# Runs of eight equal products in the half blocks, evenly issued background steps, and decay operands moved to ScalarE, in a two-layer hybrid trunk

## The chip, the cores and the metric

The kernel runs on one core of a Trainium2 chip, as one launch. The figure of merit is the device time of one execution in microseconds (us). The profile names the engines of a core: PE is TensorE (matrix products; its weight loads are listed apart as PEld), DVE is VectorE, ACT is ScalarE, POOL is GpSimd, and SP issues most of the DMA transfers. Each engine works through its own queue of instructions in order; where it needs a result of another engine, it waits on a semaphore, and everything behind the waiting instruction in its queue waits as well. PSUM is the memory into which PE accumulates.

## The reference, cut to what matters

The input is 256 tokens of 2048 features. Layer A is a gated delta-rule layer, layer B is chunked attention over the token's own chunk and the chunks before it. Both have 16 heads of 128 features, and both are wrapped the same way:

```python
# layer A (chunks of 64 tokens)
proj = h @ w_in                                   # 2048 x 8224: q, k, v, z, a, b
qkv  = silu(causal_depthwise_conv(proj[..., :6144], conv_w))
q, k = l2_norm(q) * 128 ** -0.5, l2_norm(k)
g    = -exp(a_log) * softplus(a + dt_bias);  gc = cumsum(g)      # within a chunk
decay = exp(where(tril, gc_i - gc_j, -inf))
lower = where(strict tril, (k * beta) @ k.T * decay, 0)
sol   = solve_triangular(eye + lower, [v * beta, k * beta * exp(gc)])
# a scan over the 4 chunks with a 128 x 128 state per head gives o
out   = h + (rms_norm(o) * silu(z)) @ w_out
# layer B
proj = h @ w_in                                   # 2048 x 8192: q, k, v, z
out  = h + (softmax(q @ k.T * scale + bias) @ v * silu(z)) @ w_out
```

Everything is single precision. The four weight matrices make nearly all of the arithmetic and of the traffic.

## The kernel before, in words

**Products.** PE multiplies numbers of a shorter type, fp32r. A weight `w` is therefore split into `hi = cast(w)` and `lo = w - hi`, the activations likewise into `xh` and `xl`, and a product of the reference is three on PE: hi·xh, hi·xl and lo·xh. The weights stream through the core in chunks of 512 KB, in the order of a list, `plan`. `fetch()` (L171 to L206) prepares a chunk: SP starts the transfer into `wt` (L198, four buffers), ACT casts it to `whi` (L199, three buffers), DVE subtracts to get `wlo` (L200, three buffers). A chunk is fetched three chunks ahead of its use, but a `whi` buffer can be written only when PE has done the last product that reads the chunk three before it.

**Kinds of block.** A "half" block makes 256 features for all 256 tokens from four chunks. Each chunk holds four slices (`j`) of the contraction and two sets of 128 features (`s`). For each pair (s, j) there are two products: a long one of 512 columns, hi·[xh|xl] (L247), and a short one of 256 columns, lo·xh (L250), which adds to the first half of the same accumulator. `features2` writes them in groups of two slices, four long and then four short ones. "tokens" blocks (L256 to L258) make 512 features of 256 tokens in products of 512 columns, "features" blocks (L237 to L240) in products of 256 columns. Blocks accumulate in PSUM tiles named `psp`, of which there are two buffers. When a half block is done, `joined` (L299 to L306) queues a copy of one half of it on ACT (L303) and the addition of the other half on DVE (L304); the addition frees the `psp` buffer for the block after the next.

**Order of the work.** What stands between the blocks (normalisation, convolutions, decays, the inversion of the triangular matrices, the scan, attention) is written as generators, in two lists `bgq` and `bg2`. After every slice or group the chunk loop calls `step(rate)`, which resumes one of them up to its next `yield`. A scheduler then fixes the order of each engine's queue when the kernel is built; the orders shown below are those that it fixed.

**Decays** (L392 to L494). For each of four groups of heads, `rhs` (L457 to L464) multiplies a triangular matrix by the high and the low parts of `g`: the high parts on DVE, the low parts on POOL, each one instruction of 128x512 per half. Products (L475) sum them; `tail` (L479) and three exponentials (L480, L481, L483) follow on DVE and ACT, and L490 multiplies.

**Convolution** (L494 to L505): `raw` is `ev` times a norm (L319), ACT multiplies by the first tap (L501), DVE adds the other taps (L503). **Inversion** (L596 to L697): eight copies on ACT (L610), transposes of 32x32 pieces on DVE (L620), then runs of small products on PE (L650, L670, L672). L560 are the products of keys with keys ahead of it, L706 writes a piece of the value path.

Of the kernel before, what the change touches and what calls it, by code (L numbers as in the profile page):

```python
# [23 lines left out]
NWARM = 12  # L24
TIE0 = 4
TIE = 2
GROUP = 2


C_CONV = 0  # L30
# [10 lines left out]
def tile_hybrid_trunk(  # L41
# [174 lines left out]

    turn = [0]

    def step(n=1):

        while now:
            now.pop(0)()
        for _ in range(n):
            lanes = (bgq, bg2) if turn[0] else (bg2, bgq)
            turn[0] ^= 1
            for lane in lanes:
                if advance(lane):
                    break

    def drain():  # L230
        while now or bgq or bg2:
# [7 lines left out]
        pe.matmul(ps, lhsT=hi[:, j, fs], rhs=xb[:, kt, 1, :], start=False, stop=False, skip_group_check=True)  # L239
        pe.matmul(ps, lhsT=lo[:, j, fs], rhs=xb[:, kt, 0, :], start=False, stop=(kt == KT - 1), skip_group_check=True)  # L240

    def features2(ps, hi, lo, js, ks, xb):


        both = [(s, j) for j in js for s in range(2)]
        for s, j in both:
            pe.matmul(ps[s], lhsT=hi[:, j, s * P:(s + 1) * P], rhs=xb[:, ks[j], :, :], start=(ks[j] == 0), stop=False,  # L247
                      skip_group_check=True)
        for s, j in both:
            pe.matmul(ps[s][:, 0, :], lhsT=lo[:, j, s * P:(s + 1) * P], rhs=xb[:, ks[j], 0, :], start=False,  # L250
                      stop=(ks[j] == KT - 1), skip_group_check=True)

    def tokens(ps, t, j, kt, hi, lo, xb):
        ts_ = slice(t * P, (t + 1) * P)
# [7 lines left out]
    def chunk(kind, ps, xb, rate=1, pre=None):  # L262
        i = state["use"]
        state["use"] += 1
        while state["next"] < min(i + 1 + LOOK, len(plan)):
            fetch()
        hi, lo = fetched.pop(i)
        kc = KC * 512 // plan[i][3]
        ks = [plan[i][2] * kc + j for j in range(kc)]
        f, ns = KINDS[kind]  # L270
        if kind == "half":
            ps = ps if isinstance(ps, list) else [ps[:, s] for s in range(2)]
            for j in range(0, kc, GROUP):
                js = range(j, j + GROUP)
                if pre is not None:
                    for jj in js:
                        pre(ks[jj])
                features2(ps, hi, lo, js, ks, xb)
                step(rate)
            return  # L280
        for j, kt in enumerate(ks):
            if pre is not None:
                pre(kt)
            for s in range(ns):
                f(ps[:, s], s, j, kt, hi, lo, xb)
            step(rate)

    def acc(kind):

# [104 lines left out]
    def decays():  # L394
# [61 lines left out]

        def rhs(gi):  # L457
            for half in range(2):
                for part, src in ((0, g_r), (1, gl_r)):
                    (pool if part else dve).tensor_tensor(  # L460
                        out=rbuf[:, gi % 2, 2 * half + part, :].rearrange("p (h c) -> p h c", h=4),
                        in0=lt_f.unsqueeze(1).broadcast_to([P, 4, P]),
                        in1=src[:, 4 * gi:4 * gi + 4, half].bitcast(F32).unsqueeze(2).broadcast_to([P, 4, P]),
                        op=ALU.mult)  # L464

        rhs(0)
        yield 1
# [128 lines left out]
    def inversion():  # L596
# [10 lines left out]
        for b in range(4):  # L607
            pr = slice(32 * b, 32 * b + 32)
            for t in range(2):
                act.copy(  # L610
                    out=stg[pr].rearrange("p (h t) c -> p h t c", t=2)[:, :, t, :],
                    in_=dl[pr, :, 0, T * t + 32 * b:T * t + 32 * b + 32])
            yield 1
# [31 lines left out]
        for q0 in range(0, 32, 16):  # L645
            ps = ps_small()
            for i in range(16):
                for b in (0, 2):
                    r, c = 32 * b, 32 * b + 32
                    pe.matmul(ps[c:c + 32, i * 32:(i + 1) * 32], lhsT=diag(q0 + i, r, c, 32),  # L650
                              rhs=xr[r:r + 32, q0 + i, :], start=True, stop=True, tile_position=(r, c))
            for c in (32, 96):
# [11 lines left out]
        for q0 in range(0, 32, 16):  # L664
            ps, ps2 = ps_small(), ps_small()
            for i in range(16):
                hh = q0 + i
                for b in (0, 2):
                    r, c = 32 * b, 32 * b + 32
                    pe.matmul(ps[r:r + 32, i * 32:(i + 1) * 32], lhsT=v1[c:c + 32, hh, :],  # L670
                              rhs=xt[c:c + 32, hh, :], start=True, stop=True, tile_position=(c, r))
                pe.matmul(ps2[32:64, i * 32:(i + 1) * 32], lhsT=xt[32:64, hh, :], rhs=v1[32:64, hh, :],  # L672
                          start=True, stop=True, tile_position=(32, 32))
            for r in (0, 64):
                act.copy(out=tt[r:r + 32, q0:q0 + 16, r + 32:r + 64],
                         in_=ps[r:r + 32].rearrange("p (a b) -> p a b", b=32))
# [496 lines left out]
```

## Time and profile before

| | |
|---|---|
| median of 3 runs | 1018.46 us (1017.2 to 1019.1) |
| the profiled execution | 1018.52 us |
| its span, first to last instruction | 1016.8 us |
| mean granted clock of TensorE | 0.998 |
| PE busy | 1005.7 us, 99% of the span |
| DVE busy | 695.4 us, 68% |
| ACT busy | 523.0 us, 51% |
| POOL busy | 80.0 us, 8% |

Between the profiled execution's time and its span lie 1.7 us. An engine is busy when it executes anything; the products of PE are pipelined, and the duration listed for one product is longer than the distance from its start to the start of the next. The pace of a run of products is therefore read from starts, and the time of a run of n products as the start of what follows minus the start of the run. A row of the timeline that ends in [1.77 <-ACT dl L480] says that the engine stood idle for 1.77 us before it and that ACT's line L480, writing `dl`, ended the idle time. The granted clock is given as a share of TensorE's full speed: 1.00 is 2.4 GHz, 0.50 is 1.2 GHz.

### The profile page before, as it was taken

The page shows a single profiled execution, that of the slowest core. Times are in us where ns is not written, and L with a number is a line of the kernel's source. Part 1 is how long each engine was busy: PE and PEld are TensorE (multiplying, and loading weights), DVE is VectorE, ACT ScalarE, POOL GpSimd, SP SyncE. Part 2 cuts the span into 40 slices and gives each one's busy share as a digit, 9 for nine tenths or more (in the row PEclk, how much of TensorE's full clock was granted, in tenths as well). Part 3 has the DMA queues.
Part 4 walks back from the last instruction along what each step waited for, and adds up shares of the span by engine and source line. Part 5 has one row for each costly group of instructions (what it writes and reads, how often), then busy time and mean ns, then how long its engine had stood idle before and what let it go on. Part 6 is the DMA issues. An engine that isn't in the chain of part 4 may idle for free.

```text
span 1016.8 us, 15574 instructions
## 1 busy us (share of the span) xinstructions
PE 1005.7 (99%) x6090; PEld 879.1 (86%) x6090; DVE 695.4 (68%) x1113; ACT 523.0 (51%) x724; POOL 80.0 (8%) x91
## 2 busy tenths in 40 slices
PE   8999999999999999999999999999999999999998
PEld 7987888888788989899988888888888888889987
DVE  7888889996988687755866555444456665666554
ACT  8475765555446455444654444444445555555442
POOL 2004000113000001001000000000011010101000
PEclk9999999999999999999999999999999999999999
DMA  8664665554664445545756766666665555544472
GB/s 289 183 187 115 178 184 155 156 166 146 185 190 144 108 142 149 163 145 168 246 187 187 228 207 207 188 195 196 189 186 177 153 169 163 165 154 159 158 228 90
DMA packets 134185, 177.56 MB, mean 175 GB/s; under 512 B 7904, under 2 KB 90208, under 8 KB 134112
## 3 DMA queue, kind: packets, MB, share of 16 engines
q1 hardware_dynamic: 132672, 172.12, 56.8%
q0 software_dynamic: 1152, 4.19, 1.2%
q8 instruction: 47, 0.77, 0.3%
q10 hardware_dynamic: 288, 0.26, 0.1%
q14 instruction: 26, 0.21, 0.1%
HBM read 174.46 MB, written 2.10 MB: 174 GB/s over the span
## 4 chain that ended last, share of the span: by engine, by line
PE 95%; DVE 2%; ACT 1%; issue 1%; DMA 1%; SPq 0%; ACTq 0%
PE psp L247 26%; PE psp L250 13%; PE psp L257 11%; PE psp L258 11%; PE psp L256 11%; PE psp L240 4%; PE psp L237 4%; PE psp L239 4%; PE pss L560 2%; DVE wlo L200 1%; PE pss L757 1%; PE pss L992 1%; PE pss L1011 1%; PE pss L1047 1%; PE pss L247 1%
## 5 line engine op out<-in xcount | busy, mean ns | idle before, releaser
L200 DVE TENSOR_TENSOR wlo<-wt,whi 128x1024 fp32r<-128x1024 f32 (+1 forms) x322 | 393.9, 1225 | 246.3 <-ACT whi L199 237.1
L199 ACT CAST whi<-wt 128x1024 fp32r<-128x1024 f32 (+1 forms) x322 | 336.4, 1046 | 399.3 <-PE psp L247 155.8
L247 PE MATMUL psp<-xb,whi 128*128 128x512 f32 x960 | 267.3, 397 | 0.3 <-DVE ev L304 0.3
L257 PE MATMUL psp<-wlo,xb 128*128 128x512 f32 x512 | 201.3, 393 | 1.6 <-DVE wlo L200 1.6
L258 PE MATMUL psp<-whi,xb 128*128 128x512 f32 x512 | 201.7, 394 | 0.0
L256 PE MATMUL psp<-whi,xb 128*128 128x512 f32 x512 | 200.3, 391 | 0.0
L247 PEld LDWEIGHTS psp<-xb,whi 128*128 128x128 f32 x960 | 165.1, 190 | 22.2 <-PE psp L250 0.5
L250 PEld LDWEIGHTS psp<-xb,wlo 128*128 128x128 f32 x960 | 147.9, 190 | 19.7
L250 PE MATMUL psp<-xb,wlo 128*128 128x256 f32 x960 | 156.7, 283 | 0.0
L257 PEld LDWEIGHTS psp<-wlo,xb 128*128 128x128 f32 x512 | 96.2, 188 | 21.6 <-DVE wlo L200 2.0
L256 PEld LDWEIGHTS psp<-whi,xb 128*128 128x128 f32 x512 | 96.2, 188 | 19.9 <-ACT whi L199 0.3
L258 PEld LDWEIGHTS psp<-whi,xb 128*128 128x128 f32 x512 | 96.3, 188 | 19.1
L239 PE MATMUL psp<-g,whi 128*128 128x256 f32 x256 | 73.5, 287 | 0.0
L237 PE MATMUL psp<-g,whi 128*128 128x256 f32 x256 | 73.5, 287 | 0.0
L240 PE MATMUL psp<-g,wlo 128*128 128x256 f32 x256 | 72.9, 285 | 0.0
L503 DVE SCALAR_TENSOR_TENSOR cv<-raw,sm,cv 128x254 f32<-128x254 f32 (+2 forms) x144 | 62.1, 477 | 1.8 <-ACT cv L501 1.8
L247 PE MATMUL psp<-g,whi 128*128 128x512 f32 x224 | 61.2, 395 | 0.0
L239 PEld LDWEIGHTS psp<-g,whi 128*128 128x128 f32 x256 | 49.1, 192 | 0.2
L237 PEld LDWEIGHTS psp<-g,whi 128*128 128x128 f32 x256 | 49.1, 192 | 0.1
L240 PEld LDWEIGHTS psp<-g,wlo 128*128 128x128 f32 x256 | 49.1, 192 | 0.1
L247 PEld LDWEIGHTS psp<-g,whi 128*128 128x128 f32 x224 | 38.3, 189 | 5.1
L250 PEld LDWEIGHTS psp<-g,wlo 128*128 128x128 f32 x224 | 34.4, 189 | 4.7
(248 smaller groups left out, 995.3 us busy)
## 6 DMA issues: line engine op xcount, KB each, us to landing
wt<-in_b_w_in_dram SPq DMA_DIRECT2D x128, 512.0 KB, 3.7
wt<-in_a_w_in_dram SPq DMA_DIRECT2D x127, 512.0 KB, 3.9
wt<-in_a_w_out_dram SPq DMA_DIRECT2D x32, 512.0 KB, 3.9
wt<-in_b_w_out_dram SPq DMA_DIRECT2D x32, 512.0 KB, 3.6
dl<-in_xT_dram POOLq DMA_DIRECT2D x4, 512.0 KB, 5.7
dl<-in_relb_dram POOLq DMA_DIRECT2D x4, 512.0 KB, 5.3
g<-in_xT_dram SPq DMA_DIRECT2D x7, 256.0 KB, 5.2
out_dram<-cv SPq DMA_DIRECT2D x2, 512.0 KB, 3.7
```

The source lines that it names most:

```text
L199: act.copy(out=hi[:, js, cs], in_=wt[:, js, cs])
L200: dve.tensor_tensor(out=lo[:, js, cs], in0=wt[:, js, cs], in1=hi[:, js, cs].bitcast(F32), op=ALU.subtract)
L237: pe.matmul(ps, lhsT=hi[:, j, fs], rhs=xb[:, kt, 0, :], start=(kt == 0 and s % 2 == 0), stop=False, skip_group_check=True)
L239: pe.matmul(ps, lhsT=hi[:, j, fs], rhs=xb[:, kt, 1, :], start=False, stop=False, skip_group_check=True)
L240: pe.matmul(ps, lhsT=lo[:, j, fs], rhs=xb[:, kt, 0, :], start=False, stop=(kt == KT - 1), skip_group_check=True)
L247: pe.matmul(ps[s], lhsT=hi[:, j, s * P:(s + 1) * P], rhs=xb[:, ks[j], :, :], start=(ks[j] == 0), stop=False, skip_group_check=True)
L250: pe.matmul(ps[s][:, 0, :], lhsT=lo[:, j, s * P:(s + 1) * P], rhs=xb[:, ks[j], 0, :], start=False, stop=(ks[j] == KT - 1), skip_group_chec ...
L256: pe.matmul(ps, lhsT=xh, rhs=hi[:, j, :], start=(kt == 0), stop=False)
L257: pe.matmul(ps, lhsT=xh, rhs=lo[:, j, :], start=False, stop=False)
L258: pe.matmul(ps, lhsT=xl, rhs=hi[:, j, :], start=False, stop=(kt == KT - 1))
L503: dve.scalar_tensor_tensor(out=cv[:, i, s:], in0=raw[:, i, :T - s], scalar=conv_w(i0 + i, 3 - s), in1=cv[:, i, s:], op0=ALU.mult, op1=ALU.add)
L560: pe.matmul(dst, lhsT=kq[:, a, i, c:c + P], rhs=rhs, start=(n == 0), stop=(n == 2))
```

## The change

- `features2` now writes a chunk as eight long products and eight short ones. Chunks with an even place in their block begin with the long ones, chunks with an odd place begin with the short ones, so that across chunks the order is 8 long, 16 short, 16 long, 16 short and 8 long within a block. Within a run, `s` is the outer loop and the slice `j` the inner one.
- `step` issues one step. `tick(n)` adds n to a credit and issues a step for every whole one; it is called after every four products of a half block with half the rate, and after every product group of the other kinds with a share of the rate. The hook `pre` is called once per chunk of a half block.
- The low parts of the decays' operands are made by ACT, as four activations of 128x128 each (32 in all), in place of one POOL instruction of 128x512 (8 in all).
- The inversion yields after each of its eight copies, in the middle of the first products, and after every four heads of the second ones.
- The third of the small z blocks of layer A issues its steps at rate 2 in place of 1.

The core of the difference:

```diff
-    def features2(ps, hi, lo, js, ks, xb):
-        both = [(s, j) for j in js for s in range(2)]
-        for s, j in both:
-            pe.matmul(ps[s], lhsT=hi[:, j, s * P:(s + 1) * P], rhs=xb[:, ks[j], :, :], ...
-        for s, j in both:
-            pe.matmul(ps[s][:, 0, :], lhsT=lo[:, j, s * P:(s + 1) * P], rhs=xb[:, ks[j], 0, :], ...
+    def features2(ps, hi, lo, ks, xb):
+        turns = (ks[0] // len(ks)) % 2
+        for n, long in enumerate((not turns, turns)):
+            for s in range(2):
+                for j, kt in enumerate(ks):
+                    w = (hi if long else lo)[:, j, s * P:(s + 1) * P]
+                    dst, x = (ps[s], xb[:, kt, :, :]) if long else (ps[s][:, 0, :], xb[:, kt, 0, :])
+                    pe.matmul(dst, lhsT=w, rhs=x, start=bool(long and kt == 0), stop=(n == 1 and kt == KT - 1),
+                              skip_group_check=True)
+                yield
...
+    def tick(n):
+        while now:
+            now.pop(0)()
+        credit[0] += n
+        while credit[0] >= 1:
+            credit[0] -= 1
+            step()
...
-                features2(ps, hi, lo, js, ks, xb)
-                step(rate)
+            if pre is not None:
+                pre(ks[-1])
+            for _ in features2(ps, hi, lo, ks, xb):
+                tick(rate / 2)
...
-                for part, src in ((0, g_r), (1, gl_r)):
-                    (pool if part else dve).tensor_tensor(
...
+                for i in range(4):
+                    act.activation(out=rbuf[:, gi % 2, 2 * half + 1, i * P:(i + 1) * P], in_=lt_f, func=AF.Copy,
+                                   scale=gl_r[:, 4 * gi + i, half:half + 1].bitcast(F32))
...
-        bg2.append(za_small(gi, block("tokens", xb, 1 if gi == 2 else 2)))
+        bg2.append(za_small(gi, block("tokens", xb, 2)))
```

Lines of the changed kernel stand up to 15 numbers further down: its L260 is both L247 and L250 of before, L198 and L199 are L199 and L200, L311 and L312 are L303 and L304, L327 is L319, L473 is the new activation, L490, L493 and L491 are L480, L483 and L481, L511 and L513 are L501 and L503, L539 and L541 are L529 and L531.

**PE, where one half block ends and the next begins** (near 113 us in the trace of before). Names: `psp` is the accumulator, `whi` and `wlo` the two parts of one chunk of weights, `xb` the activations. Before:

```order
L247 MATMUL psp_1213<-xb_108,whi_1215 128x512 x4
L250 MATMUL psp_1213<-xb_108,wlo_1216 128x256 x4
L247 MATMUL psp_1213<-xb_108,whi_1215 128x512 x4
L250 MATMUL psp_1213<-xb_108,wlo_1216 128x256 x4
L247 MATMUL psp_1305<-xb_108,whi_1240 128x512 x4
L250 MATMUL psp_1305<-xb_108,wlo_1241 128x256 x4
```

and now:

```order
L260 MATMUL psp_1237<-xb_108,wlo_1217 128x256 x8
L260 MATMUL psp_1237<-xb_108,wlo_1240 128x256 x8
L260 MATMUL psp_1237<-xb_108,whi_1239 128x512 x8
L260 MATMUL psp_1329<-xb_108,whi_1264 128x512 x8
L260 MATMUL psp_1329<-xb_108,wlo_1265 128x256 x8
L260 MATMUL psp_1329<-xb_108,wlo_1287 128x256 x8
```

The last products of a block are now the long ones, which read `whi`; before they were the short ones, which read `wlo`, and the last reader of `whi` stood four products earlier.

**DVE at the same place.** `wlo` is the subtraction of a chunk, `raw` and `cv` belong to the convolution, and `ev<-psp` is the addition that frees an accumulator. Before, where the block of `whi_1240` needs the buffer of `psp_1086`:

```order
L319 TENSOR_TENSOR raw_1104<-ev_1009,rB_529 128x512
L319 TENSOR_TENSOR raw_1104<-ev_1101,rB_529 128x512
L200 TENSOR_TENSOR wlo_1241<-wt_1239,whi_1240 128x1024
L503 SCALAR_TENSOR_TENSOR cv_1107<-raw_1104,sm_76,cv_1107 128x255 x2
L304 TENSOR_TENSOR ev_1228<-psp_1086,ev_1228 128x512
```

and now, where the block of `whi_1264` needs the buffer of `psp_1110`:

```order
L199 TENSOR_TENSOR wlo_1287<-wt_1285,whi_1286 128x1024
L541 TENSOR_REDUCE ssq_113<-raw_978 128x8
L327 TENSOR_TENSOR raw_1124<-ev_1029,rB_529 128x512
L327 TENSOR_TENSOR raw_1124<-ev_1121,rB_529 128x512
L199 TENSOR_TENSOR wlo_1309<-wt_1307,whi_1308 128x1024
L513 SCALAR_TENSOR_TENSOR cv_1127<-raw_1124,sm_76,cv_1127 128x255 x2
L312 TENSOR_TENSOR ev_1248<-psp_1110,ev_1248 128x512
```

Before, the last subtraction ahead of the freeing addition is that of the new block's own first chunk (`whi_1240`); now it is that of the new block's third chunk (`whi_1308`; `whi_1264` and `whi_1286` are its first and second), whose `whi` buffer is that of `whi_1239`, the chunk with which the block before ends.

**ACT in the decays** (near 80 us in the trace of before). `dl` are the exponentials, `tt` the operands of the sums. Before:

```order
L199 CAST whi_996<-wt_995 128x1024
L199 CAST whi_1021<-wt_1020 128x1024
L199 CAST whi_1043<-wt_1042 128x1024
L480 ACT_TABLE_LOAD
L480 ACTIVATE dl_112<-pss_701 128x4x128
L483 ACTIVATE dl_112<-pss_702,tail_710 128x128 x4
L481 ACTIVATE dl_112<-pss_703 128x4x128
```

and now:

```order
L198 CAST whi_1020<-wt_1019 128x1024
L198 CAST whi_1045<-wt_1044 128x1024
L473 ACTIVATE tt_684<-kT_78,gl_r_111 128x128 x16
L198 CAST whi_1067<-wt_1066 128x1024
L473 ACTIVATE tt_684<-kT_78,gl_r_111 128x128 x4
L490 ACT_TABLE_LOAD
L490 ACTIVATE dl_112<-pss_713 128x4x128
L198 CAST whi_1089<-wt_1088 128x1024
```

Twenty of the 32 new activations stand ahead of the first exponential, among the casts; the other twelve lie between the exponentials of the later groups.

In the inversion the new yields leave each of its runs together in PE's and ACT's queues: the eight copies still follow each other, and so do the products of each of its stages. Ahead of the eight copies, ACT's queue had `L706` twice and one cast behind PE's last `L560`; now it has the two only, and 32 products of the running "tokens" block follow the last `L560` up to the first that needs a chunk cast behind the copies, where 38 did.

## Rows read from the trace of the kernel before

**Rows 1.** The page's first lines, and the head of its chain of waits, the chain of work that ended last, followed back.

```profile
span 1016.8 us, 15574 instructions
...
PE 1005.7 (99%) x6090; PEld 879.1 (86%) x6090; DVE 695.4 (68%) x1113; ACT 523.0 (51%) x724; POOL 80.0 (8%) x91
...
PE 95%; DVE 2%; ACT 1%; issue 1%; DMA 1%; SPq 0%; ACTq 0%
```

**Rows 2.** Stretches of 25 us: the length, busy us and count of instructions of each engine, the granted clock of PE, the DMA share and GB/s.

```profile
75.00:100.00 25.00, 23.14 (x124) 19.34 (x124) 23.52 (x28) 13.72 (x29) 12.52 (x8) 1.00 0.41 117
...
575.00:600.00 25.00, 25.00 (x144) 21.82 (x143) 13.46 (x16) 11.38 (x12) 1.37 (x3) 1.00 0.67 209
```

**Rows 3.** The timeline of PE in a half block: start us, us, engine, line, operation, tiles, count.

```profile
300.04 1.09 PE L247 MATMUL psp<-xb,whi 128*128 128x512 f32 x4
300.97 0.63 PE L250 MATMUL psp<-xb,wlo 128*128 128x256 f32 x4
301.44 1.09 PE L247 MATMUL psp<-xb,whi 128*128 128x512 f32 x4
...
305.65 0.63 PE L247 MATMUL psp<-xb,whi 128*128 128x512 f32 x2
```

**Rows 4.** The timeline of PE where the scheduler happened to put eight long products, and a little later eight short ones, in a row.

```profile
122.81 2.02 PE L247 MATMUL psp<-xb,whi 128*128 128x512 f32 x8
124.67 0.63 PE L250 MATMUL psp<-xb,wlo 128*128 128x256 f32 x4
...
126.94 1.12 PE L250 MATMUL psp<-xb,wlo 128*128 128x256 f32 x8
127.89 1.09 PE L247 MATMUL psp<-xb,whi 128*128 128x512 f32 x4
```

**Rows 5.** The timeline of PE where a "tokens" block (512 columns) follows a half block, at its first product, its seventh and its twenty-fifth.

```profile
627.08 0.40 PE L256 MATMUL psp<-whi,xb 128*128 128x512 f32 x1
...
628.47 0.39 PE L256 MATMUL psp<-whi,xb 128*128 128x512 f32 x1
...
632.54 0.39 PE L256 MATMUL psp<-whi,xb 128*128 128x512 f32 x1
```

**Rows 6.** The timeline of PE inside a "features" block (256 columns), two products that are twelve apart.

```profile
19.95 0.28 PE L240 MATMUL psp<-xb,wlo 128*128 128x256 f32 x1
...
21.39 0.28 PE L240 MATMUL psp<-xb,wlo 128*128 128x256 f32 x1
```

**Rows 7.** The timeline of the decays, all engines.

```profile
76.50 5.04 DVE L460 TENSOR_TENSOR tt<-kT,g_r 128x512 fp32r<-128x512 f32 x4
76.75 11.10 POOL L460 TENSOR_TENSOR tt<-kT,gl_r 128x512 fp32r<-128x512 f32 x7 [39.73 <-DVE gl_r L450]
...
81.46 4.04 DVE L200 TENSOR_TENSOR wlo<-wt,whi 128x1024 fp32r<-128x1024 f32 x2
...
87.55 1.14 ACT L483 ACTIVATE dl<-pss,tail 128x128 f32<-128x128 f32 x4
...
87.70 0.74 PE L475 MATMUL pss<-tt,ones_r 128*128 128x512 f32 x2 [1.77 <-ACT dl L480]
...
94.51 0.68 DVE L460 TENSOR_TENSOR tt<-kT,g_r 128x512 fp32r<-128x512 f32 x1
```

**Rows 8.** The timeline where the half block of `psp_1305` begins, the place of the first two orders above.

```profile
111.57 1.22 DVE L200 TENSOR_TENSOR wlo<-wt,whi 128x1024 fp32r<-128x1024 f32 x1
...
112.70 0.87 DVE L503 SCALAR_TENSOR_TENSOR cv<-raw,sm,cv 128x255 f32<-128x255 f32 x2
...
113.17 1.99 ACT L199 CAST whi<-wt 128x1024 fp32r<-128x1024 f32 x2
...
113.49 0.68 DVE L304 TENSOR_TENSOR ev<-psp,ev 128x512 f32<-128x512 f32 x1
...
114.32 1.16 PE L247 MATMUL psp<-xb,whi 128*128 128x512 f32 x4 [0.33 <-DVE ev L304]
```

**Rows 9.** The timeline around the inversion's copies, inside a "tokens" block.

```profile
246.06 1.20 PE L560 MATMUL pss<-kT 128*128 128x512 f32 x6
...
247.30 1.27 ACT L706 ACTIVATE kT<-psp,rx 128x512 f32<-128x512 f32 x2 [3.31 <-PE pss L560]
...
249.39 5.03 ACT L610 COPY g<-dl 32x512 f32<-32x512 f32 x8
...
254.45 2.08 DVE L620 STREAM_TRANSPOSE g<-g 128x1024 f32<-128x1024 f32 x1 [3.13 <-ACT g L610]
...
256.45 1.19 DVE L200 TENSOR_TENSOR wlo<-wt,whi 128x1024 fp32r<-128x1024 f32 x1
...
257.69 0.50 PE L257 MATMUL psp<-wlo,xb 128*128 128x512 f32 x1 [1.64 <-DVE wlo L200]
```

**Rows 10.** Stretches of 3.4 us around the pauses of PE, with the columns of rows 2: the pause in the decays, the pause behind the inversion's copies, the inversion's own products and the stretch after them, and the end of the program.

```profile
85.70:89.10 3.40, 1.63 (x10) 1.26 (x9) 3.40 (x5) 2.05 (x7) 2.15 (x2) 1.00 0.83 257
...
255.60:259.00 3.40, 1.76 (x8) 1.23 (x8) 3.40 (x4) 1.78 (x2) 0.00 (x0) 1.00 0.08 8
...
322.40:325.80 3.40, 2.68 (x195) 2.23 (x193) 3.23 (x7) 1.71 (x3) 0.00 (x0) 1.00 0.65 174
325.80:329.20 3.40, 3.40 (x24) 2.85 (x15) 0.00 (x0) 3.31 (x6) 0.00 (x0) 0.50 0.50 144
...
1013.40:1016.80 3.40, 0.00 (x0) 0.00 (x0) 0.42 (x1) 0.00 (x0) 0.00 (x0) 0.78 0.24 80
```

More of the change, by code (lines that the diff above doesn't have):

```diff
@@ L26 @@
 TIE = 2
-GROUP = 2
 C_CONV = 0
@@ L217, in tile_hybrid_trunk, with step @@
     turn = [0]
-    def step(n=1):
+    def step():
         while now:
             now.pop(0)()
[L223 to L228, printed above, removed]
+        lanes = (bgq, bg2) if turn[0] else (bg2, bgq)
+        turn[0] ^= 1
+        for lane in lanes:
+            if advance(lane):
+                break
+    credit = [0.0]
+    def tick(n):
[5 more added lines that the diff above has]
+            step()
     def drain():
@@ L240, in features @@
         pe.matmul(ps, lhsT=lo[:, j, fs], rhs=xb[:, kt, 0, :], start=False, stop=(kt == KT - 1), skip_group_check=True)
-    def features2(ps, hi, lo, js, ks, xb):
-        both = [(s, j) for j in js for s in range(2)]
-        for s, j in both:
-            pe.matmul(ps[s], lhsT=hi[:, j, s * P:(s + 1) * P], rhs=xb[:, ks[j], :, :], start=(ks[j] == 0), stop=False,
-                      skip_group_check=True)
-        for s, j in both:
-            pe.matmul(ps[s][:, 0, :], lhsT=lo[:, j, s * P:(s + 1) * P], rhs=xb[:, ks[j], 0, :], start=False,
-                      stop=(ks[j] == KT - 1), skip_group_check=True)
+    def features2(ps, hi, lo, ks, xb):
[8 more added lines that the diff above has]
+                yield
     def tokens(ps, t, j, kt, hi, lo, xb):
@@ L272, in chunk @@
             ps = ps if isinstance(ps, list) else [ps[:, s] for s in range(2)]
[L273 to L277, printed above, removed]
-                features2(ps, hi, lo, js, ks, xb)
-                step(rate)
+            if pre is not None:
+                pre(ks[-1])
+            for _ in features2(ps, hi, lo, ks, xb):
+                tick(rate / 2)
             return
@@ L285, in chunk @@
                 f(ps[:, s], s, j, kt, hi, lo, xb)
-            step(rate)
+                tick(rate / ns)
     def acc(kind):
@@ L458, in rhs @@
             for half in range(2):
-                for part, src in ((0, g_r), (1, gl_r)):
-                    (pool if part else dve).tensor_tensor(
[L461 to L464, printed above, removed]
+                dve.tensor_tensor(
+                    out=rbuf[:, gi % 2, 2 * half, :].rearrange("p (h c) -> p h c", h=4),
+                    in0=lt_f.unsqueeze(1).broadcast_to([P, 4, P]),
+                    in1=g_r[:, 4 * gi:4 * gi + 4, half].bitcast(F32).unsqueeze(2).broadcast_to([P, 4, P]),
+                    op=ALU.mult)
+                for i in range(4):
+                    act.activation(out=rbuf[:, gi % 2, 2 * half + 1, i * P:(i + 1) * P], in_=lt_f, func=AF.Copy,
+                                   scale=gl_r[:, 4 * gi + i, half:half + 1].bitcast(F32))
         rhs(0)
@@ L612, in inversion @@
                     in_=dl[pr, :, 0, T * t + 32 * b:T * t + 32 * b + 32])
-            yield 1
+                yield 1
         xbf = xb.rearrange("p a b -> p (a b)")
@@ L651, in inversion @@
                               rhs=xr[r:r + 32, q0 + i, :], start=True, stop=True, tile_position=(r, c))
+                if i == 7:
+                    yield 1
             for c in (32, 96):
@@ L673, in inversion @@
                           start=True, stop=True, tile_position=(32, 32))
+                if i % 4 == 3 and i < 15:
+                    yield 1
             for r in (0, 64):
```

## Prediction

> **What bounds the kernel now.** I read the page's busy times first, then its chain of waits, then stretches of 25 us, and then the timeline where a stretch shows PE below full. PE is busy for 1005.7 of 1016.8 us and holds 95% of the chain [rows 1]: PE is the bound. The stretch from 575 shows how most of the program looks, PE full, while ACT and DVE have half of the time free [rows 2]. So only two kinds of change count: another pace of PE's products, and another wait in front of them. The stretch from 75 is one of the few with a wait: DVE is nearly full there, and PE has only 23.14 of 25 us [rows 2]. The timeline names three waits that the change touches: 1.77 us before the products of the decays [rows 7], 0.33 us before the half block at 114.3 [rows 8], and 1.64 us in the "tokens" block at 257.7 [rows 9]. The clock is full except for one stretch behind the inversion's products, and at the end [rows 10].
>
> **Runs of eight.** The change makes no product more or less: 1208 long and 1208 short ones, 75.5 times sixteen of each. Now, four groups of four long and four short take 305.65 − 300.04 = 5.61 us, and four long take 0.93, 0.232 each; four short 0.47, 0.118 each [rows 3]. Steady runs elsewhere show what a longer run may settle at: 18 products of 512 columns from the seventh to the twenty-fifth take 632.54 − 628.47 = 4.07, 0.2265 each, but the first six after short products take 1.39, 0.232 each [rows 5]. Products of 256 columns settle at 1.44 / 12 = 0.120, a little slower than the 0.118 of a group of four [rows 6]. The run of eight long products takes 124.67 − 122.81 = 1.86, the run of eight short ones 127.89 − 126.94 = 0.95; together 2.81, just two groups of four and four [rows 4]. So the first eight of a run win nothing, and only what follows them can: sixteen long take 1.86 + 8 × 0.2265 = 3.67, sixteen short 0.47 + 12 × 0.120 = 1.91, together 5.58 in place of 5.61. That is 0.03 × 75.5 = 2.4 us (estimate). The bounds: nothing, by the runs of eight, and with every long product at 0.2265 and the short ones kept at 0.1175, 16 × (0.232 − 0.2265) = 0.09, some 7 us. I take 2.4, being nearest to runs of the lengths that are made.
>
> **Decays.** PE waits there for an exponential, which comes late because DVE is late: four L460 take 5.04 us beside POOL's own, and one alone takes 0.68, and two L200 take 4.04 beside POOL where one takes 1.22 elsewhere [rows 7, 8]. The change takes POOL out. DVE's four L460 fall to about 2.7, its L200 to about 1.2 each, and the exponentials can start several us earlier. The price is 32 activations on ACT. Four of the same width take 1.14 [rows 7], so 32 take 9.1, and the twenty ahead of the first exponential 5.7. ACT has 25 − 13.72 = 11.3 us free in that stretch [rows 2]. Sixteen of them in a row hold the cast behind them up by 4.6; PE needs 2.8 for a chunk [rows 3], and chunks are fetched three ahead, so the cover is some 8. It could fail at one cast, for up to 0.6 us (estimate). I take the wait as gone, −1.8 (1.77 in the row), within −1.8 and −1.2; nothing below excludes that it stays whole, which would give 0.
>
> **The boundary between two half blocks at 113 us.** The order shows a closed chain. The first product of the new block waits for the addition that frees an accumulator (L312); that stands in DVE's queue behind the subtraction of the new block's third chunk; the cast of that chunk writes the buffer of `whi_1239`, and that is read by the very last products before the boundary, since an odd chunk now ends with its long products. Nothing of this can run ahead. PE is therefore idle for the whole of it: about 0.16 from PE's last start to the cast's release (estimate), a cast of 1.00, a subtraction of 1.22 (it starts with the cast's end, and 1.15 is the pitch of two), two taps of 0.87 together, the addition of 0.68, and a few hundredths at each handoff: 3.9 us in all [rows 8]. It takes the place of the wait that is there now, 0.33 in the row, 0.4 to 0.5 by the starts of the products. Behind the waiting product PE has nothing else to do: all that follows in its queue waits too. So +3.9 and −0.4. Bounds: 3.2 if one of the links is shorter, 4.5 if the first tap's activation on ACT stands in the way too. A boundary near 540 us has a similar chain with one chunk more of cover: 0.16 + 1.00 + 1.2 + 0.7 and handoffs are 3.2, against 2.8 for a chunk's products [rows 3]: +0.4, between 0 and 0.6.
>
> **The inversion's copies.** They stay together, so the chain does too. Now it runs from the last L560 at 247.26 to the product at 257.69: L706 twice (1.27), a cast, the copies (5.03), the transposes (2.08), a subtraction (1.19) [rows 9]: 10.4 us, of which 38 products cover 38 × 0.2265 = 8.6 [rows 5, 9]. After, one cast of 1.0 less stands before the copies, so some 9.6, and 32 products cover 7.25. The wait is 2.3 in place of 1.9: +0.4 (0 to 1).
>
> **The clock.** Pauses of PE of 1.6 to 1.8 us left it at 1.00 (PE 1.63 and 1.76 busy of 3.40). After the stretch with the inversion's 195 small products it was at 0.50 for 3.4 us, and at the end, without products, it fell as well [rows 10]. A pause of 3.9 us is twice as long as those that did no harm. I take it that the clock falls to half once after it. In 3.4 us at half 1.7 are lost; part of that time may lie in the pause itself, so 1.3 (0 to 1.7).
>
> **Evenly issued steps** move work of DVE and ACT between places where PE is full and they are half free [rows 2]; I cost this at nothing beyond the waits above, which the order gives.
>
> The sum: 1018.52 − 2.4 − 1.8 − 0.4 + 3.9 + 0.4 + 0.4 + 1.3 = 1019.9. The profiled execution lies 0.06 from the median of 1018.46, so nothing is corrected for that.
>
> **Rivals.**
> A. Runs bring nothing: the rows of eight say so [rows 4], the steady 0.2265 of the "tokens" blocks against it [rows 5]. Then 1019.9 + 2.4 = 1022.3. The Trainium skill, "TensorE: Matmul & The Clock Gate", section "Back-to-back issue gap", has the distance of two products depend on their columns, columns / 2.4 ns and 2.5 more when isolated, and on the weight load in a stream; which width stood before doesn't enter. By that rule the order inside a block buys nothing, and this rival holds. The trace doesn't bear it out: products of the same 512 columns with the same kind of load take 0.232 or 0.2265, where the formula has 0.216.
> B. The clock falls a second time, behind the pause in the "tokens" block, which grows to 2.3 us: 1019.9 + 1.6 = 1021.5. For it speaks that the pause is longer than any that is harmless now; against it that the harmless ones are only a little shorter [rows 10].
> C. The other side, faster: long products settle at 0.2265 from the first on, and short ones keep their 0.1175. The gain is 7 in place of 2.4: 1015.3, and 1014.0 if the clock holds as well. It decides from 0.06 saved per sixteen of each. Against it speak the first six after short products, and 0.120 in steady runs [rows 5, 6].
> D. The clock does not fall at 113 us, or the fall behind the inversion's products goes too, since the work around these moves: 1019.9 − 1.3 = 1018.6, with both 1018.6 − 1.7 = 1016.9.
> E. The chain at the boundary isn't closed, because a link runs earlier than I read: 1019.9 − 3.9 − 1.3 = 1014.7. The order of the queues and the three buffers of `whi` speak against it.
>
> **How the numbers follow.** My forecast is 1019.9, with 0.45; its own range is 1018.3 to 1021.3. A has 0.15, B 0.15, C 0.07, D 0.13, E 0.05. The range of 1016.5 to 1022.8 takes in the forecast, A, B and D with their tails, and leaves out C and E and a little above, less than 2 in 10. A difference of 0.2%, 2.0 us, is about what a measurement of this kernel can tell from no change: under 1016.4 is faster, over 1020.5 slower. C and E make faster 0.12. A and B and the upper quarter of the forecast's range are slower: 0.15 + 0.11 + 0.15 = 0.41. The rest, 0.47, is the same.
>
> **What would show it.** The pause before the first product of a half block near 110 us, ended by DVE's L312, 3 to 4.5 us long; under 1 us and the chain was misread. No pause before the products of the decays, and the high parts on DVE (L467 now) at 0.7 each. Sixteen long products in 3.67 and sixteen short ones in 1.91. A pause of 2 to 2.5 us behind the copies (L620), near 250 us. A granted clock of 0.50 in a stretch of 3.4 us behind the pause at the boundary. A new pause of over 1 us elsewhere, before a product that waits for a cast in the decays above all, would make the forecast wrong, and so would a pace outside 5.51 to 5.62 per sixteen of each.

## Result and the profile after

The changed kernel takes 1022.58 us (median of 7 executions, 1018.85 to 1025.31), the kernel before 1017.33 us on the same chip (7 executions, 1016.75 to 1019.1). The ratio is 1.0047, with a 95% interval of 1.0028 to 1.0067: slower by half a per cent. The profiled execution took 1021.71 us, 3.2 more than that of before.

The head of the page (span, busy times, chain of waits), beside [rows 1]:

```profile
span 1020.0 us, 15627 instructions
...
PE 1005.8 (99%) x6090; PEld 882.6 (87%) x6090; DVE 689.0 (68%) x1113; ACT 532.5 (52%) x756; POOL 65.9 (6%) x83
...
PE 97%; DVE 1%; issue 1%; DMA 1%; ACT 0%; SPq 0%; DVEq 0%
```

PE's busy time is that of before to 0.1 us, but busy time counts a product at half clock as work. What PE waited for stands in the view of waits (total us, times, the longest):

```profile
PE psp L260 <- DVE ev L312: 4.4, 2, 4.1
PE pss L684 <- issue: 1.7, 1, 1.7
PE psp L268 <- DVE wlo L199: 1.6, 1, 1.6
...
PE psp L267 <- ACT whi L198: 0.4, 1, 0.4
```

Two of these are new or grown: 4.1 us for the addition that frees an accumulator, and 1.7 us for "issue", which is an engine that waits for nothing the profile shows. The wait of 1.77 us in the decays [rows 7] is gone. The clock is the third difference. Stretches of 3.41 us behind the two waits, with the columns of rows 2, and the stretch of the decays:

```profile
75.00:100.00 25.00, 25.00 (x136) 21.63 (x135) 18.12 (x28) 23.96 (x59) 0.00 (x0) 1.00 0.53 147
...
116.40:119.81 3.41, 3.41 (x12) 2.87 (x12) 3.41 (x9) 0.94 (x1) 0.00 (x0) 0.50 0.31 110
119.81:123.22 3.41, 3.41 (x22) 3.03 (x22) 1.55 (x2) 2.57 (x4) 0.00 (x0) 1.00 0.16 17
...
321.20:324.61 3.41, 2.52 (x30) 2.10 (x31) 1.47 (x3) 1.94 (x5) 0.00 (x0) 0.50 0.79 229
324.61:328.02 3.41, 3.41 (x17) 3.07 (x16) 1.28 (x3) 1.81 (x3) 0.00 (x0) 0.50 0.00 0
328.02:331.43 3.41, 3.41 (x61) 3.41 (x61) 2.29 (x4) 0.00 (x0) 0.00 (x0) 1.00 0.00 0
```

PE is at half clock for 10.2 us, where before it was for 3.4 [rows 10]. The first row shows PE full in the decays now, and ACT busy for 23.96 of 25 us, where it was for 13.72 [rows 2].

The sum for the profiled execution: the wait at the boundary 4.15 − 0.33 = +3.8; the decays −1.8; "issue" 1.74 − 0.72 = +1.0; half clock +3.0 (1.7 at 116; at 321 there are 6.83 − 0.88 of idle time, half of it is 3.0, against 1.7 before); the "tokens" block 0.35 + 1.61 − 1.64 = +0.3; the start +0.4; a wait of 0.2 near 564; the runs −3.4 if they go at their steady pace everywhere (below). Together +3.5, measured +3.2. By an experiment below the runs are worth about 2 us and not 3.4; with that the sum is +4.9, and some 1.7 us too much stand in the other terms. Half clock is the likeliest of them, since it is priced as if every product in it took twice as long; this is not shown.

The other executions differ from this one in the clock. Sorted by their mean granted clock, the changed kernel's seven give 1018.85 us at 0.997, 1020.79 and 1021.71 at 0.995, 1022.58 at 0.993, 1023.23 and 1024.81 at 0.992, 1025.31 at 0.990. Where the clock fell is recorded for the profiled execution alone; the means show that equal work, in an equal order, loses more time to it in some executions than in others.

### The profile page after: what moved, and what is told of

The parts are those of the page before. It is cut to its first block, busy times and chain, and to the rows that moved or that the text cites. A ratio compares the mean times of both kernels' runs of the same rounds, so it can differ in the third digit from the quotient of the medians.

```text
span 1020.0 us, 15627 instructions
## 1 busy us (share of the span) xinstructions
PE 1005.8 (99%) x6090; PEld 882.6 (87%) x6090; DVE 689.0 (68%) x1113; ACT 532.5 (52%) x756; POOL 65.9 (6%) x83
## 4 chain that ended last, share of the span: by engine, by line
PE 97%; DVE 1%; issue 1%; DMA 1%; ACT 0%; SPq 0%; DVEq 0%
PE psp L260 40%; PE psp L268 11%; PE psp L269 11%; PE psp L267 11%; PE psp L249 4%; PE psp L248 4%; PE psp L246 4%; PE pss L570 2%; PE pss L260 1%; PE pss L771 1%; PE pss L1006 1%; PE pss L1025 1%; PE pss L1061 1%; PE pss L485 1%; DMA g<-in_xT_dram 1%
## 5 line engine op out<-in xcount | busy, mean ns | idle before, releaser
L199 DVE TENSOR_TENSOR wlo<-wt,whi 128x1024 fp32r<-128x1024 f32 (+1 forms) x322 | 391.3, 1217 | 247.1 <-ACT whi L198 240.6
L198 ACT CAST whi<-wt 128x1024 fp32r<-128x1024 f32 (+1 forms) x322 | 336.4, 1046 | 386.2 <-PE psp L269 148.8
L260 PE MATMUL psp<-xb,whi 128*128 128x512 f32 x960 | 238.4, 395 | 4.4 <-DVE ev L312 4.4
L260 PEld LDWEIGHTS psp<-xb,whi 128*128 128x128 f32 x960 | 176.3, 190 | 38.7 <-DVE ev L312 5.2
L260 PEld LDWEIGHTS psp<-xb,wlo 128*128 128x128 f32 x960 | 127.4, 193 | 5.7
L260 PE MATMUL psp<-xb,wlo 128*128 128x256 f32 x960 | 132.3, 286 | 0.0
L513 DVE SCALAR_TENSOR_TENSOR cv<-raw,sm,cv 128x255 f32<-128x255 f32 (+2 forms) x144 | 62.3, 474 | 2.7 <-ACT cv L511 2.4
L260 PE MATMUL psp<-g,whi 128*128 128x512 f32 x224 | 53.8, 391 | 0.0
L248 PEld LDWEIGHTS psp<-g,whi 128*128 128x128 f32 x256 | 49.1, 192 | 0.2
L246 PEld LDWEIGHTS psp<-g,whi 128*128 128x128 f32 x256 | 49.1, 192 | 0.1
L249 PEld LDWEIGHTS psp<-g,wlo 128*128 128x128 f32 x256 | 49.1, 192 | 0.1
L260 PEld LDWEIGHTS psp<-g,whi 128*128 128x128 f32 x224 | 41.1, 188 | 7.8
L260 PEld LDWEIGHTS psp<-g,wlo 128*128 128x128 f32 x224 | 28.7, 191 | 1.1
```

What stands on the lines that cost most here:

```text
L198: act.copy(out=hi[:, js, cs], in_=wt[:, js, cs])
L199: dve.tensor_tensor(out=lo[:, js, cs], in0=wt[:, js, cs], in1=hi[:, js, cs].bitcast(F32), op=ALU.subtract)
L246: pe.matmul(ps, lhsT=hi[:, j, fs], rhs=xb[:, kt, 0, :], start=(kt == 0 and s % 2 == 0), stop=False, skip_group_check=True)
L260: pe.matmul(dst, lhsT=w, rhs=x, start=bool(long and kt == 0), stop=(n == 1 and kt == KT - 1), skip_group_check=True)
L513: dve.scalar_tensor_tensor(out=cv[:, i, s:], in0=raw[:, i, :T - s], scalar=conv_w(i0 + i, 3 - s), in1=cv[:, i, s:], op0=ALU.mult, op1=ALU.add)
```

## The experiments

Ratios are against the kernel before on the same chip; medians of different chips are not quite comparable (that of before went from 1017.24 to 1018.54 us). The waits and "half", the time at 0.50 with the end of the program left out, are those of one execution, the profiled one. In `low_on_act`, `runs_alone`, `wt3`, `shift38`, `ev3` (both times), `ev3_fours` and `ev3_copies`, 3.4 us of "half" lie near 12 us, behind the waits of the start, which all kernels have; in the others the clock did not fall there.

| kernel | median us | ratio, 95% interval | decays | boundary | "issue" | half |
|---|---|---|---|---|---|---|
| before | 1017.33 | | 1.77 | 0.33 | 0.72 | 3.4 |
| changed | 1022.58 | 1.0047 (1.0028 to 1.0067) | none | 4.15 | 1.74 | 10.2 |
| low_on_act | 1023.52 | 1.0058 (1.0043 to 1.0074) | none | 3.69 | 2.24 | 10.2 |
| runs_alone | 1022.49 | 1.0052 (1.0038 to 1.0066) | 2.10 | none | 3.07 | 13.7 |
| low_on_pool | 1022.55 | 1.0042 (1.0027 to 1.0057) | 1.76 | none | 3.85 | 13.7 |
| ev3 | 1012.08 | 0.9949 (0.9934 to 0.9963) | none | none | none | 3.4 |
| ev3 again | 1012.35 | 0.9948 (0.9933 to 0.9963) | none | none | none | 3.4 |
| wt3 | 1022.12 | 1.0039 (1.0023 to 1.0055) | none | 4.64 | 1.69 | 10.2 |
| shift128 | 1017.73 | 0.9992 (0.9982 to 1.0003) | none | 4.15 | none | 6.8 |
| shift38 | 1018.95, one run | | none | 4.17 | 0.53 | 6.8 |
| before_shift | 1017.73 | 0.9993 (0.9982 to 1.0004) | 1.77 | none | none | 6.8 |
| ev3_fours | 1013.93 | 0.9960 (0.9946 to 0.9975) | none | none | 0.27 | 3.4 |
| ev3_pool_s | 1015.71 | 0.9986 (0.9976 to 0.9997) | 1.76 | none | none | 3.4 |
| ev3_copies | 1009.88 | 0.9922 (0.9910 to 0.9935) | none | none | none | 3.4 |

### What makes the wait at the boundary

`low_on_act` is the kernel before with the low parts on ACT, `runs_alone` the kernel before with the runs; `low_on_pool` is the changed kernel with the low parts on POOL again:

```diff
-    (pool if part else dve).tensor_tensor(...)      # low_on_act: this alone; low_on_pool: all but this
+    act.activation(out=rbuf[...], in_=lt_f, func=AF.Copy, scale=gl_r[...])
```

> The kernel before with one part of the change alone: the decays' low parts on ACT instead of POOL. Theory A (the run order makes the pause at the boundary near 112 us, since a block now ends with the products that read whi): no pause over 0.6 us there, the pause of 1.77 us in the decays gone, 1017.3 - 1.8 = 1015.5 us. Theory B (moving the low parts makes it: PE arrives earlier, ACT is full in the decays, so the addition that frees the accumulator is late, with groups of four as well): a pause of 3 to 4 us near 112 us ended by L304, the clock at 0.50 once behind it, 1017.3 - 1.8 + 3.3 + 1.7 = 1020.5 us.

> The kernel before with the runs of eight long and eight short products alone (steps after every eight products, as many per chunk as before). Both theories: the addition stands in DVE's queue behind the subtraction of the new block's first chunk, as before, so no new pause; the pause in the decays stays at about 1.8 us. It measures the runs: 0.045 us per sixteen of each by the starts of the blocks in the changed kernel's trace, times 75.5 = 3.4 us, 1013.9 us. If runs bring nothing by themselves, 1017.3 us.

> The changed kernel with the decays' low parts back on POOL. Theories A and B: the addition stands behind the new block's first chunk's subtraction, so the pause near 112 us is under 1 us and the clock doesn't fall there, while the pause of 1.8 us in the decays is back: 1022.6 - 4.2 - 1.7 + 1.8 = 1018.5 us by the median, less where the clock falls less often, 1015 to 1018.5. A rival, C (most of the loss is the clock behind the inversion's products, where it fell for 6.8 in place of 3.4 us): 1021 us or more.

The wait goes with the low parts and not with the runs. `low_on_act` has it with groups of four, 3.69 us; `runs_alone` and `low_on_pool` have none there. In `runs_alone` the addition is done before PE, in the middle of sixteen long products, comes to the new block (its first product is the ninth of the sixteen, at 116.36):

```profile
114.36 0.69 DVE L305 TENSOR_TENSOR ev<-psp,ev 128x512 f32<-128x512 f32 x1
...
114.52 3.82 PE L251 MATMUL psp<-xb,whi 128*128 128x512 f32 x16
```

The timeline of `low_on_act` shows the chain:

```profile
112.74 1.05 ACT L199 CAST whi<-wt 128x1024 fp32r<-128x1024 f32 x1 [1.11 <-PE psp L247]
...
114.20 1.22 DVE L200 TENSOR_TENSOR wlo<-wt,whi 128x1024 fp32r<-128x1024 f32 x1
...
116.13 0.69 DVE L304 TENSOR_TENSOR ev<-psp,ev 128x512 f32<-128x512 f32 x1
...
116.87 1.29 PE L247 MATMUL psp<-xb,whi 128*128 128x512 f32 x4 [3.69 <-DVE ev L304]
```

The changed kernel has the same chain:

```profile
111.55 1.04 ACT L198 CAST whi<-wt 128x1024 fp32r<-128x1024 f32 x1 [1.05 <-PE psp L260]
111.79 1.29 DVE L327 TENSOR_TENSOR raw<-ev,rB 128x512 f32<-128x512 f32 x2
...
113.00 1.22 DVE L199 TENSOR_TENSOR wlo<-wt,whi 128x1024 fp32r<-128x1024 f32 x1
113.33 0.56 ACT L311 COPY ev<-psp 128x512 f32<-128x512 f32 x1
...
114.13 0.87 DVE L513 SCALAR_TENSOR_TENSOR cv<-raw,sm,cv 128x255 f32<-128x255 f32 x2
...
114.92 0.68 DVE L312 TENSOR_TENSOR ev<-psp,ev 128x512 f32<-128x512 f32 x1
...
115.66 3.17 PE L260 MATMUL psp<-xb,whi 128*128 128x512 f32 x8 [4.15 <-DVE ev L312]
```

In both, the cast waited for PE's last product with the buffer, and the subtraction, the taps and the addition follow one upon the other until PE may go on. What the runs add is that the last reader of that buffer is the block's very last product, four short products later than in groups of four: 4.15 − 3.69 = 0.46 us, and four short products take 0.47 [rows 3].

The gain expected of the other two did not come, though the wait was absent: both are some 5 us slower than before. Theory C, the rival in the third expectation, was right of them: "issue" holds PE for 3.07 and 3.85 us, and at its end or just behind it the clock falls, for 6.8 and 10.2 us. In `low_on_pool`:

```profile
324.70 0.26 PE L680 MATMUL pss<-g 32*32 32x32 f32 x1 [3.85 <-issue]
```

and the stretches behind it:

```profile
324.48:327.89 3.41, 3.19 (x57) 2.48 (x58) 1.08 (x3) 2.09 (x4) 0.00 (x0) 0.50 0.21 72
327.89:331.30 3.41, 3.41 (x27) 3.19 (x26) 1.39 (x2) 0.69 (x1) 0.00 (x0) 0.50 0.00 0
331.30:334.71 3.41, 3.41 (x9) 2.18 (x9) 0.23 (x1) 1.04 (x1) 0.00 (x0) 0.50 0.00 0
```

### A third buffer for `ev`

```diff
-            ev = work.tile([P, 2, T], F32, name="ev", tag="ev")
+            ev = work.tile([P, 2, T], F32, name="ev", tag="ev", bufs=3)
-        wt = wst.tile([P, kc, width], F32, name="wt", tag="wt", bufs=4)
+        wt = wst.tile([P, kc, width], F32, name="wt", tag="wt", bufs=3)
```

`wt3` has the second edit alone.

> The changed kernel with three ev buffers in place of two, and three wt buffers in place of four to make room. The addition near 112 us then stands ahead of the new block's own subtractions in DVE's queue. If the closed chain is what holds it: no pause over 0.6 us there, no fall of the clock there, 1022.6 - 4.2 - 1.7 = 1016.7 us. If the addition is late for the work of the convolution in front of it: a pause of 1.5 to 3 us remains, 1018 to 1021 us.

> The changed kernel with three wt buffers in place of four, and two ev buffers as it had: the control to ev3. If the third ev buffer is what ev3 owes its time to: the pause near 112 us stays at 4 us, the idle time at instruction 4034 at 1.7 us, 1021.5 to 1024 us. If it was the weights' transfers, started otherwise by the third wt buffer: under 1018 us.

`ev3` is faster than before by 0.5%, twice, and PE waits neither at the boundary nor in the inversion's products. Its stretches:

```profile
100.00:125.00 25.00, 25.00 (x150) 22.09 (x150) 22.15 (x31) 18.61 (x32) 0.00 (x0) 1.00 0.60 171
...
300.00:325.00 25.00, 25.00 (x314) 21.86 (x314) 24.50 (x40) 15.46 (x20) 2.08 (x2) 1.00 0.58 166
```

The control, `wt3`, keeps both waits:

```profile
PE psp L260 <- DVE ev L312: 4.9, 2, 4.6
PE pss L684 <- issue: 1.7, 1, 1.7
```

In its profiled execution the clock was at 0.50 for 6.8 us behind the boundary, and did not fall behind the 1.69 us of "issue".

So the accumulator was held because its contents had nowhere to go: with two `ev` buffers the copy that comes before the addition must wait until the convolution has read the last pair (above, L327 at 111.79 and the copy, L311, at 113.33). With a third, the addition no longer stands behind the new block's subtractions: it is at 102.71 in `ev3`, whose new block begins at 112.49. That the third buffer takes the wait away is shown; that the scheduler put the addition where it did for the sake of that copy is argued from the order. `ev3` gains 10.5 us on the changed kernel by the medians, 10 by the ratios, more than the 5.9 of the wait and one fall of the clock: "issue" and the falls behind it are gone as well, and that was no aim of the edit (next section).

### Where "issue" comes from

If every weight load, product and semaphore instruction that the trace has for PE is numbered in order of time, the idle time in before, the changed kernel, `low_on_act`, `runs_alone` and `low_on_pool` lies at number 4033 or 4034 each time, though the product that waits is another one in each. So it does in `wt3` (1.69 us), `shift38` (0.53) and `ev3_fours` (0.27). The same trace has transfers of an instruction queue, 16,384 bytes each, about one per 256 instructions of PE. One lands 1.3 to 1.6 us before the idle time ends, in all five; in `low_on_pool` it only starts at 322.23, when PE has stood idle since 320.85. The transfers of the changed kernel between 319.4 and 321 us, the moment at which PE stops:

```profile
q8 instruction: 1, 0.02, 5.1%
```

and PE there:

```profile
320.09 0.25 PE L682 MATMUL pss<-g 32*32 32x32 f32 x4
322.08 0.26 PE L684 MATMUL pss<-g 32*32 32x32 f32 x1 [1.74 <-issue]
```

The inversion's products of 32x32 run through PE's instructions much faster than any other stretch: some 255 instructions of L660 took 2.0 us (311.52 to 313.55 in the changed kernel), where half blocks need more than 20 us for as many. My theory F: PE has used up one block of instructions before the next is there. How far the run of small products has come by then depends on where it begins: the second one begins at number 3779 in before, 3702 in the changed kernel and 3830 in `ev3`, which has no idle time. It can be tested by moving the stream and leaving the order of all other work as it is, with short products in place of some of those that PE runs ahead of everything; `shift128` does it thus, `shift38` and `before_shift` in the same way:

```diff
-    for _ in range(NWARM):
+    for _ in range(NWARM - 4):
         pe.matmul(ps, lhsT=warm[:, :P], rhs=warm, start=True, stop=True)
+    for _ in range(68):
+        pe.matmul(ps[:, 0:16], lhsT=warm[:, :P], rhs=warm[:, 0:16], start=True, stop=True)
```

> The changed kernel with eight of the twelve warm-up products and 68 short ones of 16 columns more, so that 128 instructions more stand in PE's stream ahead of everything else; the order of all other work is that of the changed kernel. Theory F (PE's idle time inside the inversion's small products lies at one place of its stream, instruction 4034, where a block of 16 KB of instructions ends and the next has not arrived; how long it is depends on where the run of small products begins): the run begins at 3830 in place of 3702, as in ev3, so the idle time of 1.74 us is gone and the clock doesn't fall behind it, while the pause of 4.2 us near 112 us stays: 1022.6 - 1.7 - 1.7 to 3.4 = 1017.5 to 1019.2 us, plus up to 0.8 for the start. If the idle time has another cause (the copies, the weights' transfers), it stays at 1.5 to 2 us: 1022.6 us or a little more.

> As shift128, with 38 instructions more in PE's stream: the run of small products begins at 3740, as in low_on_pool and runs_alone. Theory F: the idle time at instruction 4034 grows from 1.7 to 3 to 4 us, with the clock at 0.50 for 6.8 us or more behind it. Otherwise it stays at 1.5 to 2 us.

> The kernel before with 52 more instructions of short warm-up products ahead of everything, so that the inversion's second run of small products begins at 3831 of PE's stream in place of 3779. Theory F: the idle time of 0.72 us at instruction 4034 is gone, and in those executions in which the clock fell behind it, 1.7 us more: 1016 to 1017.5 us, 1 to 2 us less than before. Else: as before, or up to 0.5 more for the start.

`shift128` takes the idle time away and with it the falls of the clock behind it. The ratio goes from 1.0047 to 0.9992, while the wait at the boundary stays at 4.15 us, here with 6.8 us of half clock behind it. That leaves the boundary as the chief difference to `ev3`, which has no "issue" either: 0.9992 against 0.9949, some 4.4 us. The stretch of the inversion:

```profile
300.00:325.00 25.00, 25.00 (x450) 22.08 (x449) 22.90 (x35) 17.17 (x24) 2.09 (x2) 1.00 0.58 168
```

`shift38`, a single run, missed: the idle time stayed at number 4034, but 0.53 us long and not 3 to 4. In `low_on_pool` the second run of small products begins at the same number; there 40 instructions stand between the two runs of small products, in `shift38` 56. Where these 56 are the same (the changed kernel, `wt3`, `shift38`, `shift128`), the later the second run begins the shorter the idle time: 1.74 and 1.69 us from 3702, 0.53 from 3740, none from 3830. That goes with theory F. The place is fixed by the stream, then; what else sets the length was not settled. `before_shift` missed in its time: the 0.72 us are gone, but the median is that of before. In its profiled execution the clock fell behind two other waits, in the decays and in the "tokens" block.

### What the parts are worth without the waits

> The kernel ev3 (the changed one with three ev and three wt buffers) with half blocks in groups of four long and four short products again. No pause near 112 us in either. If the runs are worth 0.045 us per sixteen of each, it is 3.4 us slower than ev3, 1015.5 us, up to 1 more for an idle time at instruction 4034 (the small products begin at 3802, between before and ev3). If runs bring nothing by themselves, as the rows of eight had it: 1012.1 to 1013 us.

`ev3_fours` is `ev3` with four long and four short products in turn. It is 1.85 us slower by the medians, by ratios of 0.9960 and 0.9949 about 1.1; in both profiled executions the clock fell once, at the start, and the last product ends 3.4 us later, of which 0.8 lie in a wait at the start and 0.27 in "issue". That leaves 2.3, so the runs are worth about 2 us. Their pace in the changed kernel:

```profile
588.13 2.08 PE L260 MATMUL psp<-xb,wlo 128*128 128x256 f32 x16
590.04 3.82 PE L260 MATMUL psp<-xb,whi 128*128 128x512 f32 x16
593.70 2.08 PE L260 MATMUL psp<-xb,wlo 128*128 128x256 f32 x16
```

Sixteen short ones take 590.04 − 588.13 = 1.91 us, sixteen long ones 593.70 − 590.04 = 3.66, together 5.57, against 5.61 [rows 3]. From block to block it is 0.045 us less per sixteen of each where nothing else runs; that in all 75.5 would be 3.4 us, but other work breaks into the runs in layer A.

> The kernel ev3 with the decays' low parts back on POOL, and with 88 more instructions of short warm-up products, so that the inversion's second run of small products begins at 3830 of PE's stream as in ev3 and no idle time arises there. It prices the move of the low parts by itself: the pause of 1.8 us in the decays is back, with a fall of the clock behind it in some runs: 1012 + 1.8 + 0 to 1.7 = 1013.8 to 1015.5 us. If the move is worth nothing by itself: 1012 to 1013 us.

`ev3_pool_s` is 3.4 us slower than `ev3` on the same chip: the wait of 1.76 us in the decays is back, and in the profiled execution the clock is at 0.50 behind it from 88.8 to 92.2. The added warm-up is no part of it: the same early product starts at 12.09 us, and at 12.04 in `ev3`. How the rest splits is not shown.

The other parts of the change (evenly issued steps, the inversion's yields, the rate of the z block) were never run by themselves. `low_on_pool`, which has them and the runs, ends within 0.1 us of `runs_alone`, but "issue" differs between the two.

### A better version

`ev3_copies` is `ev3` with every second copy of the inversion on DVE:

```diff
-                act.copy(
+                (dve.tensor_copy if t else act.copy)(
                     out=stg[pr].rearrange("p (h t) c -> p h t c", t=2)[:, :, t, :],
```

> The kernel ev3 with four of the inversion's eight copies on DVE in place of ACT. If the copies on ACT, which hold up the casts behind them, make the waits of 1.9 us near 256 us: those are under 0.6 us, 1012 - 1.4 to 1.9 = 1010.3 us. If DVE's own work there (the transposes, 2.1 us) makes them: 1.5 to 2 us remain, 1012 us.

```profile
249.82 2.51 ACT L620 COPY g<-dl 32x512 f32<-32x512 f32 x4
250.46 1.27 DVE L620 COPY g<-dl 32x512 f32<-32x512 f32 x3
252.09 0.42 DVE L620 COPY g<-dl 32x512 f32<-32x512 f32 x1
...
252.62 2.12 DVE L630 STREAM_TRANSPOSE g<-g 128x1024 f32<-128x1024 f32 x1
```

The copies are done in 2.5 us in place of 5.03 [rows 9], and PE waits for nothing in that block. 1009.88 us is 2.5 less than `ev3` on the same chip, of which the wait that is gone makes 1.6; it beats both kernels, by 0.8% that of before.

## Why the prediction was right, and where it was wrong

The time lies in the range, by 0.2 us, and 2.7 us above the 1019.9 forecast; the kernel is slower where "the same" had the largest chance, at 0.47 against 0.41. Part of this is luck. The sum set out from 1018.52, and before measured 1017.33 beside the change: the forecast is a loss of 1.4 us, the medians lose 5.2 and the profiled executions 3.2. The sum has the wait at the boundary and the decays right, but half clock is 1.7 us too small in it and "issue" is missing; the upper end of the range was drawn for rivals A and B and takes these in by chance. One of the prediction's own signs of being wrong came up too, a "new pause of over 1 us elsewhere": "issue" is 1.74 us and was 0.72.

**The runs** came out as worked out: 3.66 and 1.91 for the 3.67 and 1.91 of the steady rows, and some 2 us in all for 2.4. (Two slips change next to nothing: 0.03 × 75.5 is 2.3 and not 2.4, and 4.07 / 18 is 0.2261 and not 0.2265.) Rival A (nothing) and rival C (7 us) are both out. The Trainium skill, "TensorE: Matmul & The Clock Gate", section "Back-to-back issue gap", lets the distance of two products go by their columns and, in a stream, the weight load. That does not hold to the last per cent here: with the same columns and the same kind of load it is 0.229 per long product in a run of sixteen, 0.232 in groups of four.

**The decays** came out too, with the wait gone. The four instructions on DVE that took 5.04 us beside POOL take 2.49, and ACT's sixteen take 4.80, for the 4.6 of the estimate:

```profile
77.64 2.49 DVE L467 TENSOR_TENSOR tt<-kT,g_r 128x512 fp32r<-128x512 f32 x4
77.75 4.80 ACT L473 ACTIVATE tt<-kT,gl_r 128x128 fp32r<-128x128 f32 x16 [0.28 <-DVE gl_r L458]
```

**The boundary** had the right size, 4.15 for 3.9 us, and the right chain, but the step named the wrong cause: "an odd chunk now ends with its long products. Nothing of this can run ahead." `runs_alone` has those products and no wait; `low_on_act` has the wait without them. It is the earlier and heavier decays that put the addition behind the new block's third subtraction, and two `ev` buffers that let them; the runs make it 0.46 us longer. The second boundary, priced at 0.4 near 540 us, has no wait at 540; the one wait of this kind after it is 0.21 us, at 563.92, behind a cast, a subtraction and an addition as described there.

**The clock** is the step that failed in size: "I take it that the clock falls to half once after it." It did fall there, but behind the inversion's products it stayed low for 6.8 us in place of 3.4, and by their mean clocks the other executions lost less or more to it. Rival B had a further fall, but in the "tokens" block. And pauses "that did no harm" was read from a single execution: behind the same 1.76 to 2.10 us in the decays the clock was at 0.50 in the profiled executions of `runs_alone`, `low_on_pool`, `ev3_pool_s` and `before_shift`.

**"Issue"** was missing from the sum. Before had 0.72 us of it, in the stretch whose clock fell [rows 10]; I priced the inversion's yields by the order, found them without effect, and did not see that a change in the number of PE's instructions ahead of that stretch changes how long it is. That is +1.0 us, and 1.3 more of half clock.

**The "tokens" block** came out near: 0.35 and 1.61, together 1.96 us, for 2.3, and 0.3 more than before for 0.4.

## What to carry to other kernels

When an accumulator is freed late, look at what the freeing instruction itself waits for: here one more small buffer for the copied-out result took away a wait of 4.15 us, of which the freeing addition itself is 0.68. Where a saving ends one wait, follow the earlier engine to the next place at which it must wait for the slower chain. And in a kernel whose main engine is always busy, an idle stretch can have a second price in the clock, which one execution pays and another does not; so compare executions by their granted clock before a cause is given to a difference of 1 to 3 us.

## What was not expected of the hardware

Tiny products, it seems, can run PE out of instructions. The idle time lay at the same number of PE's instruction stream in eight kernels, 0.27 to 3.85 us long; moving the stream by 128 instructions took it away and brought the median from 1.0047 to 0.9992 of before. That the next instructions were late is argued, from the place and from the transfer that lands just ahead of its end; no run held up such a transfer by itself. The Trainium skill, "Runtime: NRT & Kernel Launch", section "Instruction fetch mechanics", says that instructions come in blocks of 16 KiB and that crossing a block is mostly hidden. The trace agrees on the blocks (16,384 bytes); with products of 32x32 the crossing was not hidden here.
